# Delta rule's block inverse: products over 64 changed columns, whole array at every level, sixteens stored in both orientations

## The chip, the cores and the metric

The kernel runs on one core of a Trainium2 chip. The metric is device microseconds of one execution, the median of several runs. The engines are named as in the profile: PE is TensorE's matmul stream, PEld its weight loads, DVE is VectorE, ACT is ScalarE, POOL is GpSimd, SP is the engine that issues most DMAs. ACT issues the others.

## What is computed

A two-layer encoder over 512 tokens of width 2048. Layer 0 projects the tokens to six heads of neighbourhood attention, six heads of a bidirectional gated delta rule and four heads that attend to 256 memory tokens; it gates, concatenates and projects back. Layer 1 does the same with differential attention. The change touches only the delta rule, and in it only the solve with a triangular matrix:

```python
def gated_delta_rule_chunked(q, k, v, g, beta):      # chunks of 64 tokens
    ...
    a_mat = jnp.where(lower_strict, jnp.einsum('bhnid,bhnjd->bhnij', kb, k) * decay, 0.0)
    rhs = jnp.concatenate([v * beta[..., None], kb * jnp.exp(G)[..., None]], axis=-1)
    sol = lax.linalg.triangular_solve(a_mat + jnp.eye(C, dtype=f32), rhs, left_side=True, lower=True)
    ...
    def step(S, xs):
        v_new = u_c - jnp.einsum('bhcd,bhde->bhce', w_c, S)
        o = jnp.einsum('bhcd,bhde->bhce', qd_c, S) + jnp.einsum('bhij,bhje->bhie', qk_c, v_new)
        S = S * ge[..., None, None] + jnp.einsum('bhcd,bhce->bhde', kd_c, v_new)
```

The backward direction is the same on the flipped sequence. The kernel takes chunks of 128 tokens in place of 64 (four of them, TT = 4) and builds the inverse of I + A for each.

## The kernel before

The projections are the bulk: weights come in as float32, are split by ACT and DVE into a high and a low part (tiles wh and wl), and every projection is three matmuls. Everything else is "side work": generators that wait in five lanes. After each slot of a projection, `Lanes.step` lets the front entries of each lane emit one step, if by the planner's own count of engine time (class `Clock`) their operands are due:

```python
for e in list(q[0]):
    if e[1] + LAG > c.t["pe"]:
        continue
    c.due = 0.0
    if next(e[0], None) is None:
```

PE executes strictly in the order in which the program emits its matmuls and transposes (`MANUAL` names PE alone); the other engines' order is set by the framework's scheduler. So a side product whose operand is late holds up the projections behind it on PE.

For each delta head h, `dn_prep` (lane 2) makes A for both directions, writes it to DRAM (tile a_d), reads the 16 by 16 diagonal blocks back with one block on each partition, inverts them row by row on DVE, writes the inverses to DRAM (x_d), and reads them back as block-diagonal 128 by 128 matrices, one 128x512 tile for each direction. Then `dn_levels` (lane 4, both directions in turn) doubles the inverted blocks from 16 to 32 to 64 to 128: with N the inverse so far and Mm its transpose, N is replaced by N - Mm' (A' N masked to the new blocks). Each level needs the transpose of N (`tr4`, four PE transposes into a PSUM tile, and a copy by ACT), two sets of four products, a DVE multiply by the level's mask (tile lv, two masks for each direction) and a DVE subtraction. `mm4` does the four products at full size, 128 columns each; the last level uses 64 by 64 operands on a quarter of the array. Which of N and Mm comes from DRAM and which by transposition differs by direction, so each direction starts with a `tr4` of the tile that was loaded. `dn_rec` (lane 0) then runs the recurrence over the four chunks.

All matmuls of the block inverse are in plain float32, while the projections use fp32r. A float32 matmul stands in the trace as two MATMUL records and two LDWEIGHTS records; a transpose, or an fp32r matmul, stands as one. In a name like `pa<-w,w` the moving operand comes first, the stationary one second; the form gives the stationary size, then the output.

`zero_scratch` clears x_d once, with DMAs from SP behind which the loads of weights queue; `make_eye` fills a constant.

Of the kernel before, what the change touches and what calls it, by code (L numbers as in the profile page):

```python
# [14 lines left out]
P = 128  # L15
# [71 lines left out]
class WStream:  # L87
    """The weights in the order of their use, each unit loaded and split ahead of it."""

# [71 lines left out]
class Clock:  # L161
    """A rough count of each engine's time and of when each tile is written, so that side work is emitted
    when its operands are due."""

# [45 lines left out]
class Lanes:  # L210
    """Side work, advanced step by step between the slots of the projections."""

# [37 lines left out]
def tile_hybrid(ctx: ExitStack, tc: tile.TileContext, xT, memT, we, wo, wek, wok, weo, woo, vecs, rows, rpb,  # L250
# [63 lines left out]
    act(early, mhalf[:, 0:1], AF.Copy)  # L314
    # the array's clock rises with activity: keep it busy while the first operands come in
    warm = w2()
# [73 lines left out]

# [1 line left out]
    def run(gen):  # L392
        """Emit a projection with a step of side work behind each of its slots."""
        while True:
            try:
                next(gen)
            except StopIteration as e:
                clock.due = 0.0
                return e.value
            lanes.step()  # L400

    def chunk(hi, lo, nt, hook=None):
        """Tokens on the partitions, the weights' columns on the free axis."""
        n = W.width()
        per = 2 if n <= 256 else 1
        full = [pb() for _ in range(nt // per)]
        banks = [full[t // per][:, (t % per) * n:(t % per + 1) * n] for t in range(nt)]
        done = 0
        for k, wh, wl in W.ks():
            if hook is not None and k + 2 < KT:  # L410
                hook(k + 2)
            for t in range(nt):
                xh, xl = hi(k, t), lo(k, t)
                mm(banks[t], xh, wh, start=(k == 0 and t % per == 0), stop=False)
                mm(banks[t], xh, wl, start=False, stop=False)
                mm(banks[t], xl, wh, start=False, stop=(k == KT - 1 and t % per == per - 1))
                done += n
                if done >= SLOT and (k < KT - 1 or t < nt - 1):
                    done = 0
                    yield  # L420
        return banks

    def group(hi, lo, order=range(KT), hook=None):
        """The weights' columns on the partitions, tokens on the free axis."""
        ps = pb()
        for i, wh, wl in W.ks():
            k = order[i]
            if hook is not None:
                hook(i)
            mm(ps, wh, hi[k], start=(i == 0), stop=False)  # L430
            mm(ps, wh, lo[k], start=False, stop=False)
            mm(ps, wl, hi[k], start=False, stop=(i == KT - 1))
            if i % GS == GS - 1 and i < KT - 1:
                yield
        return ps
# [40 lines left out]

# [1 line left out]
    xh, xl = [], []  # L478
# [8 lines left out]

    # the squares follow behind the operands that the first products wait for
    late = []
# [113 lines left out]
    def mem_attention(xh, xl, rs, gq, kv, keep, hook=None):  # L603
        """rs() gives the tokens' rstd, kv() the keys and values, once the chunk has been emitted."""
        banks = run(chunk(lambda k, t: xh[k][:, t * P:(t + 1) * P], lambda k, t: xl[k][:, t * P:(t + 1) * P], 4, hook))
# [89 lines left out]

# [1 line left out]
    mix = [None] * KT  # L697
# [4 lines left out]
    def keep(i, f):  # L702
        """An output of layer 0 waits in DRAM for its gate, unless that is near."""
        if i in (5, 10, 11):
            mix[i] = f
        else:
            nc.sync.dma_start(mix_d[:, i, :], f)
            parked[i] = mix_d[:, i, :]
# [33 lines left out]
    def na_task(h, raws, vh, vl, xb):  # L742
# [7 lines left out]
        kh, kl = transposed([raws[t][:, P:2 * P] for t in range(TT)], V("na_k"))  # L750
        # relative position bias, over the scale
        tb = xb
# [6 lines left out]
        for i in range(3):  # L759
            qs = slice(64 + 128 * i, 192 + 128 * i)  # L760
            ks = slice(128 * i, 128 * i + 256)
            blocks.append((i // 2, slice((i % 2) * M, (i % 2 + 1) * M), P, qs, ks, slice(0, 256)))
        # the last eight columns of the grid, then the first eight
        for j in range(2):
# [48 lines left out]

# [1 line left out]
    NH = 12  # L815
# [14 lines left out]
    def delta_gates():  # L830
        load_ba()
        yield 1
        def t24(name):
# [5 lines left out]
                          op=ALU.add)  # L839
        # log1p(exp(-|y|)), with the rounding of 1 + e put back  # L840
        vec.scalar_tensor_tensor(ab, yb, -1.0, yb, op0=ALU.mult, op1=ALU.max)
# [41 lines left out]

    # conv weights over two (the silu takes x/2)
    cw = const.tile([P, 90], F32, name="cw")
# [48 lines left out]

    # The diagonal blocks of 16 of I + A, each on a partition: forward substitution, row by row.
    # The scratch rows of a chunk are 129 * 128 apart, so that every block is 16 * 129 after the one before.
    CS = 129 * P
    a_d = [dram.tile([2 * TT * CS], F32, name=f"a_d{i}") for i in range(2)]
    x_d = [dram.tile([2 * TT * CS], F32, name=f"x_d{i}") for i in range(2)]

# [6 lines left out]
    def zero_scratch():  # L947
        z = w2()
        nc.gpsimd.memset(z, 0.0)
        for x in x_d:  # L950
            for d in range(2):
                nc.sync.dma_start(rows_ap(x, d), v3(z, 4))

    eye16 = const.tile([64, 256], F32, name="eye16")

    def make_eye():
        nc.gpsimd.memset(eye16, 0.0)
        nc.gpsimd.memset(eye16[:, 0:256:17], 1.0)

    def dn_head(h):  # L960
# [10 lines left out]
    def dn_prep(b):  # L971
# [83 lines left out]
        for i in range(1, 16):  # L1055
            tmp = w2()[0:64, 0:i * i].rearrange("p (c j) -> p c j", c=i)
            row = g[:, 16 * i:16 * i + i].unsqueeze(1).to_broadcast([64, i, i])
            vec.tensor_tensor(tmp, row, x3[:, 0:i, 0:i], op=ALU.mult)
            vec.tensor_reduce(x[:, 16 * i:16 * i + i], tmp, AX.X, ALU.add, negate=True)
        yield 1  # L1060
        dma(blocks_ap(xd), x.rearrange("p (i j) -> p i j", i=16))
        yield 1
        inv = []
        for d in range(2):
            r = w2()
            dma(v3(r, 4), rows_ap(xd, d))
            inv.append(r)
        yield 1
        b.inv = inv

    def dn_levels(b, d):
        while b.inv is None:
            yield 1
        A = b.a[d]
        # backward, the blocks come transposed
        ips = tr4(b.inv[d])
        other = w2()
        copy(other, ips)
        N, Mm = (other, b.inv[0]) if d == 0 else (b.inv[1], other)
        for li in range(2):  # L1080
            yield 1
            if li > 0:
                mps = tr4(N)
                Mm = w2()
                copy(Mm, mps)
            pps = mm4(A, N)
            Pm = w2()
            vec.tensor_tensor(v3(Pm, 4), v3(pps, 4), cm(lv[:, d, li, :]), op=ALU.mult)
            yield 1
            nps = mm4(Mm, Pm)  # L1090
            vec.tensor_tensor(N, N, nps, op=ALU.subtract)
        yield 1
        # last level: the block between the two halves
        lo_, hi_ = slice(0, 64), slice(64, 128)
        a, c_ = (lo_, hi_) if d == 0 else (hi_, lo_)
        mps = tr4(N)
        Mm = w2()
        copy(Mm, mps)
        pps = pb()
        A4, N4, M4, p4 = v3(A, 4), v3(N, 4), v3(Mm, 4), v3(pps, 4)  # L1100
        for t in range(TT):
            mm(p4[a, t, c_], A4[c_, t, a], N4[c_, t, c_], start=True, stop=True)
        Pm = w2()
        P4 = v3(Pm, 4)
        copy(P4[a, :, c_], p4[a, :, c_])
        yield 1
        nps = pb()
        n4 = v3(nps, 4)
        for t in range(TT):
            mm(n4[a, t, c_], M4[a, t, a], P4[a, t, c_], start=True, stop=True)  # L1110
        vec.tensor_tensor(N4[a, :, c_], N4[a, :, c_], n4[a, :, c_], op=ALU.subtract)
        yield 1
# [97 lines left out]
    make_eye()  # L1210
    # masks of the doubling levels
    lv = const.tile([P, 2, 2, P], mybir.dt.bfloat16, tag="lv", name="lv")
# [12 lines left out]

    # lambda
    lp = small(2)
# [11 lines left out]

    # rotary tables times the gains: [c1 | c2] and [-s2 | s1]  # L1240
    tabs = []
# [14 lines left out]

    # out projection, residual, and the operands of layer 1
    x1_d = dram.tile([P, KT, T], F32, name="x1_d")
# [16 lines left out]

# [1 line left out]
    mix1 = [None] * KT  # L1277
# [155 lines left out]
def _layout(inputs):  # L1433
# [47 lines left out]
    def bias(first, rows_, cols):  # L1481
        """Partition (a, r), free (b, rk): the table at row difference rk - r, column difference from first + b - a."""
        a_, b_ = np.arange(rows_)[:, None, None, None], np.arange(cols)[None, None, :, None]
# [69 lines left out]
```

## Time and profile before

| | |
|---|---|
| runs | 2022.9, 2024.73, 2024.98 us; median 2024.73 |
| span of the profiled execution, first to last instruction | 2021.8 us |
| median less that span | 2.9 us |
| instructions | 27331 |

The profiled execution shows its span; what lies around the instructions is the difference to the runs, about 1 to 3 us. In the rows below, L263 is the line of every `mm`, L333 of every transpose, L205 of every DVE, ACT or POOL operation, and L340 of every DMA that ACT issues for the side work; groups are therefore told apart by tile and form.

### The profile page before, as it was taken

Reading aid. Unit: us, or ns where it says so; the run is one execution under the profiler, and the core shown is the slowest. Engines: PE = TensorE matmul, PEld = TensorE weight load, DVE = VectorE, ACT = ScalarE, POOL = GpSimd, SP = SyncE. Lnnn points to the kernel's source line nnn. Section 1 sums busy time; section 2 is a strip of 40 time slices with the busy share of each in tenths; the row PEclk is TensorE's granted clock in tenths of the full one; section 3 lists DMA queues with packets and bytes.
Section 4 is the critical chain, followed back from the end, with each engine's and each line's share of the span. In section 5 each row is a group of like instructions: output and inputs, shape, how many; then the busy total and the mean of one; then the engine's idle time right before and its main releaser. Section 6 shows DMA issues by size and latency. Waiting matters only on the chain.

```text
span 2021.8 us, 27331 instructions
## 1 busy us (share of the span) xinstructions
PE 2002.1 (99%) x10843; PEld 1741.7 (86%) x10843; DVE 1155.9 (57%) x2147; ACT 759.7 (38%) x1334; POOL 129.8 (6%) x124
## 2 busy tenths in 40 slices
PE   9999999999999999999999999999999999999999
PEld 7988899998988888888888889889899898888887
DVE  6676676767585766445334456566465656345222
ACT  5555344433343343324223343433434334223211
POOL 0100020201020202000000000100001000000000
PEclk9999999999999999999999999999999999999999
DMA  6454432222322233233444322122221222223332
GB/s 214 155 166 171 133 99 89 89 91 89 97 85 91 90 100 112 85 106 126 146 141 140 129 75 77 60 93 75 74 84 64 83 84 73 94 94 130 141 141 89
DMA packets 97503, 216.09 MB, mean 107 GB/s; under 512 B 21808, under 2 KB 36448, under 8 KB 97376
## 3 DMA queue, kind: packets, MB, share of 16 engines
q1 hardware_dynamic: 67776, 201.16, 29.1%
q10 hardware_dynamic: 29600, 13.19, 2.5%
q8 instruction: 85, 1.39, 0.3%
q14 instruction: 42, 0.34, 0.1%
HBM read 196.81 MB, written 17.51 MB: 106 GB/s over the span
## 4 chain that ended last, share of the span: by engine, by line
PE 96%; DVE 2%; DMA 1%; issue 1%; POOL 0%; ACT 0%; ACTq 0%; SPq 0%; DVEq 0%; POOLq 0%
PE pa L263 92%; PE pa L333 4%; DVE w L205 1%; DMA w<-in_xT_dram 0%; DMA w<-in_lvl_dram 0%; DVE s L205 0%; DMA w<-x_d 0%; POOL w L205 0%; DVE wl L205 0%; DVE vn L205 0%; POOL s L205 0%; DVE vb L205 0%; DVE S L205 0%; ACT wh L205 0%; ACT vd L205 0%
## 5 line engine op out<-in xcount | busy, mean ns | idle before, releaser
L205 ACT ACTIVATE wh<-wr 128x1024 fp32r<-128x1024 f32 (+3 forms) x333 | 341.7, 1027 | 720.5 <-PE pa L263 529.2
L205 DVE TENSOR_TENSOR wl<-wr,wh 128x1024 fp32r<-128x1024 f32 (+3 forms) x333 | 397.4, 1194 | 311.5 <-ACT wh L205 310.7
L263 PE MATMUL pa<-hi,wh 128*128 128x512 f32 x1312 | 518.1, 395 | 0.0
L263 PE MATMUL pa<-hi,wl 128*128 128x512 f32 x1312 | 511.6, 390 | 0.0
L263 PE MATMUL pa<-lo,wh 128*128 128x512 f32 x1312 | 511.3, 390 | 0.0
L263 PE MATMUL pa<-wh,hi 128*128 128x512 f32 (+3 forms) x1280 | 450.0, 352 | 2.4 <-ACT wh L205 2.4
L263 PE MATMUL pa<-wl,hi 128*128 128x512 f32 (+3 forms) x1280 | 439.5, 343 | 0.1
L263 PE MATMUL pa<-wh,lo 128*128 128x512 f32 (+3 forms) x1280 | 439.1, 343 | 0.0
L263 PEld LDWEIGHTS pa<-hi,wl 128*128 128x128 f32 x1312 | 246.4, 188 | 51.6
L263 PEld LDWEIGHTS pa<-hi,wh 128*128 128x128 f32 x1312 | 246.6, 188 | 49.1 <-DVE vb L205 0.5
L263 PEld LDWEIGHTS pa<-lo,wh 128*128 128x128 f32 x1312 | 246.7, 188 | 48.3
L263 PEld LDWEIGHTS pa<-wh,hi 128*128 128x128 f32 x1280 | 243.2, 190 | 23.2 <-ACT wh L205 3.2
L263 PEld LDWEIGHTS pa<-wh,lo 128*128 128x128 f32 x1280 | 242.8, 190 | 20.5
L263 PEld LDWEIGHTS pa<-wl,hi 128*128 128x128 f32 x1280 | 243.3, 190 | 19.2 <-DVE wl L205 0.6
L263 PE MATMUL pa<-w,w 128*128 128x256 f32 (+5 forms) x1416 | 191.9, 283 | 2.5 <-DVE w L205 1.6
L205 ACT ACTIVATE w<-pa 128x512 f32<-128x512 f32 (+4 forms) x234 | 123.2, 549 | 188.4 <-PE pa L333 134.6
L263 PEld LDWEIGHTS pa<-w,w 128*128 128x128 f32 (+2 forms) x1416 | 172.7, 181 | 17.1 <-issue 3.6
L205 DVE TENSOR_TENSOR w<-pa,w 128x512 fp32r<-128x512 f32 (+2 forms) x108 | 71.3, 679 | 147.9 <-PE pa L263 108.2
L205 POOL TENSOR_TENSOR s<-s,mhalf 128x1 f32<-128x1 f32 (+3 forms) x58 | 68.6, 1182 | 1190.8 <-DVE s L205 1187.8
L205 ACT ACTIVATE w<-w 128x512 f32<-128x512 f32 (+3 forms) x207 | 112.5, 578 | 55.1 <-DVE w L205 45.2
L205 ACT ACTIVATE w<-pa,s 128x256 f32<-128x256 f32 (+1 forms) x104 | 58.7, 570 | 128.8 <-DVE s L205 112.7
L333 PE MATMUL pa<-ct,w 128*128 128x128 f32 x712 | 100.4, 273 | 3.1 <-DMA w<-x_d 2.5
(148 smaller groups left out, 1461.0 us busy)
## 6 DMA issues: line engine op xcount, KB each, us to landing
wr<-in_wo_dram SPq DMA_DIRECT2D x112, 512.0 KB, 3.2
wr<-in_we_dram SPq DMA_DIRECT2D x75, 512.0 KB, 3.3
wr<-in_weo_dram SPq DMA_DIRECT2D x32, 512.0 KB, 3.2
wr<-in_woo_dram SPq DMA_DIRECT2D x32, 512.0 KB, 3.2
wr<-in_we_dram SPq DMA_DIRECT2D x40, 384.0 KB, 3.0
w<-in_xT_dram SPq DMA_DIRECT2D x32, 256.0 KB, 4.5
wr<-in_wek_dram SPq DMA_DIRECT2D x16, 512.0 KB, 4.1
wr<-in_wok_dram SPq DMA_DIRECT2D x16, 512.0 KB, 3.4
```

Of the source, the lines that this page charges most:

```text
L205: return f(*a, **k)
L263: nc.tensor.matmul(o, lhsT, rhs, start=start, stop=stop)
L333: nc.tensor.transpose(o, i, ident if idn is None else idn)
```

## The change

The inverse blocks of 16 are written to DRAM twice, as they are and transposed (x_d becomes two pairs of arrays; ACT makes the transposed copy xt), and each direction loads both N and Mm. The first `tr4` and its copy go. At every level only the 64 columns that change are multiplied: the half of N's column blocks that takes part, gathered by the access pattern `half`. The last level uses the whole 128 by 128 stationary operand like the others, and its mask is a scale of 0 or 1 for each partition (tile halves) in ACT's copy. The scratch to be cleared doubles, from four DMAs to eight. The diff also drops comments; without those:

```diff
-    x_d = [dram.tile([2 * TT * CS], F32, name=f"x_d{i}") for i in range(2)]
+    x_d = [[dram.tile([2 * TT * CS], F32, name=f"x_d{i}{j}") for j in range(2)] for i in range(2)]
...
-        for x in x_d:
+        for x in x_d[0] + x_d[1]:
             for d in range(2):
                 nc.sync.dma_start(rows_ap(x, d), v3(z, 4))
...
+    halves = const.tile([P, 2], F32, name="halves")
...
+        nc.gpsimd.memset(halves, 0.0)
+        nc.gpsimd.memset(halves[0:64, 0:1], 1.0)
+        nc.gpsimd.memset(halves[64:128, 1:2], 1.0)
...
-        yield 1
-        dma(blocks_ap(xd), x.rearrange("p (i j) -> p i j", i=16))
+        xt = w2()[0:64, 0:256]
+        copy(xt.rearrange("p (j i) -> p i j", i=16), x.rearrange("p (i j) -> p i j", i=16))
+        yield 1
+        for src, x_ in ((x, xd[0]), (xt, xd[1])):
+            dma(blocks_ap(x_), src.rearrange("p (i j) -> p i j", i=16))
         yield 1
         inv = []
         for d in range(2):
-            r = w2()
-            dma(v3(r, 4), rows_ap(xd, d))
-            inv.append(r)
+            pair = []
+            for x_ in (xd[1 - d], xd[d]):
+                r = w2()
+                dma(v3(r, 4), rows_ap(x_, d))
+                pair.append(r)
+            inv.append(pair)
...
-        ips = tr4(b.inv[d])
-        other = w2()
-        copy(other, ips)
-        N, Mm = (other, b.inv[0]) if d == 0 else (b.inv[1], other)
-        for li in range(2):
+        N, Mm = b.inv[d]
+        for li, s in enumerate((16, 32, 64)):
             yield 1
             if li > 0:
                 mps = tr4(N)
                 Mm = w2()
                 copy(Mm, mps)
-            pps = mm4(A, N)
+            def half(a, t=None):
+                a = a if t is None else a[:, t * P:(t + 1) * P]
+                return a.rearrange("p (k two s) -> p k two s", two=2, s=s)[:, :, 1 - d, :]
+            def split_cols(ap, n):
+                return ap.rearrange("p (k s) -> p k s", k=n)
+            pps = pb()
+            for t in range(TT):
+                mm(split_cols(pps[:, t * 64:(t + 1) * 64], 64 // s), A[:, t * P:(t + 1) * P], half(N, t),
+                   start=True, stop=True)
             Pm = w2()
-            vec.tensor_tensor(v3(Pm, 4), v3(pps, 4), cm(lv[:, d, li, :]), op=ALU.mult)
-            yield 1
-            nps = mm4(Mm, Pm)
-            vec.tensor_tensor(N, N, nps, op=ALU.subtract)
-        yield 1
-        lo_, hi_ = slice(0, 64), slice(64, 128)
-        a, c_ = (lo_, hi_) if d == 0 else (hi_, lo_)
-        mps = tr4(N)
-        Mm = w2()
-        copy(Mm, mps)
...
-            mm(p4[a, t, c_], A4[c_, t, a], N4[c_, t, c_], start=True, stop=True)
...
-            mm(n4[a, t, c_], M4[a, t, a], P4[a, t, c_], start=True, stop=True)
-        vec.tensor_tensor(N4[a, :, c_], N4[a, :, c_], n4[a, :, c_], op=ALU.subtract)
+            if li < 2:
+                m = half(lv[:, d, li, :]).unsqueeze(1).to_broadcast([P, TT, 64 // s, s])
+                vec.tensor_tensor(Pm[:, 0:256].rearrange("p (t k s) -> p t k s", t=TT, s=s),
+                                  pps[:, 0:256].rearrange("p (t k s) -> p t k s", t=TT, s=s), m, op=ALU.mult)
+            else:
+                copy(Pm[:, 0:256], pps[:, 0:256], halves[:, d:d + 1])
+            yield 1
+            nps = pb()
+            for t in range(TT):
+                c = slice(t * 64, (t + 1) * 64)
+                mm(nps[:, c], Mm[:, t * P:(t + 1) * P], Pm[:, c], start=True, stop=True)
+            vec.tensor_tensor(half(N), half(N), split_cols(nps[:, 0:256], 256 // s), op=ALU.subtract)
```

## Rows read from the trace of the kernel before

**Rows 1.** The page's head: span, and busy time of PE.

```profile
span 2021.8 us, 27331 instructions
...
PE 2002.1 (99%) x10843; PEld 1741.7 (86%) x10843; DVE 1155.9 (57%) x2147; ACT 759.7 (38%) x1334; POOL 129.8 (6%) x124
```

**Rows 2.** The chain that ended last, shares of the span by engine.

```profile
PE 96%; DVE 2%; DMA 1%; issue 1%; POOL 0%; ACT 0%; ACTq 0%; SPq 0%; DVEq 0%; POOLq 0%
```

**Rows 3.** Busy time by stretch: the six delta heads, 210 to 900 us.

```profile
210.00:900.00 690.00, 680.67 (x4036) 607.77 (x4035) 460.41 (x973) 262.83 (x506) 82.56 (x70) 1.00 0.30 94
```

**Rows 4.** PE groups by shape: busy us, mean ns of one record, idle before.

```profile
L263 PE MATMUL pa<-w,w 128*128 128x128 f32 x438 | 55.6, 275 | 0.0
...
L263 PE MATMUL pa<-w,w 64*64 64x64 f32 x192 | 16.2, 225 | 0.0
...
L263 PE MATMUL pa<-ct,w 128*128 128x1 f32 x48 | 5.8, 242 | 0.0
```

**Rows 5.** Timeline of weight loads: start, length of the run, count.

```profile
255.22 0.97 PEld L263 LDWEIGHTS pa<-ct,w 128*128 128x128 f32 x8
...
325.09 0.97 PEld L263 LDWEIGHTS pa<-w,w 128*128 128x128 f32 x8
...
329.46 0.54 PEld L263 LDWEIGHTS pa<-w,w 64*64 64x64 f32 x8 [0.17 <-issue]
```

**Rows 6.** The chain in order of time, 540 to 680 us: start, length, what.

```profile
627.52 0.44 PE pa L333 x4
627.96 0.89 PE pa L263 x8
```

**Rows 7.** PE's timeline around one set of last-level products, head 0.

```profile
331.54 0.34 PE L263 MATMUL pa<-wl,hi 128*128 128x384 f32 x1
331.72 0.34 PE L263 MATMUL pa<-wh,lo 128*128 128x384 f32 x1
331.99 0.68 PE L263 MATMUL pa<-w,w 64*64 64x64 f32 x8
...
332.87 0.34 PE L263 MATMUL pa<-wl,hi 128*128 128x384 f32 x1
```

**Rows 8.** Waits of PE, 210 to 900 us: total us, times, longest.

```profile
PE pa L333 <- DMA w<-x_d: 2.5, 2, 2.3
PE pa L263 <- DVE s L205: 2.4, 2, 1.2
PE pa L263 <- DVE vn L205: 2.4, 2, 1.6
```

**Rows 9.** DVE and ACT groups by shape, columns as in rows 4.

```profile
L205 ACT ACTIVATE w<-pa 128x512 f32<-128x512 f32 x110 | 64.4, 596 | 119.4 <-PE pa L333 82.3 <-PE pa L263 36.9
...
L205 DVE TENSOR_TENSOR w<-pa,lv 128x512 f32<-128x512 f32 x24 | 16.4, 689 | 23.8 <-PE pa L263 23.8
...
L205 DVE TENSOR_TENSOR w<-w,pa 64x256 f32<-64x256 f32 x12 | 5.0, 419 | 18.2 <-PE pa L263 18.2
```

**Rows 10.** DMA issues: queue, count, KB each, median us to landing.

```profile
w<-x_d ACTq DMA_DIRECT2D x12, 256.0 KB, 4.2
...
x_d<-w ACTq DMA_DIRECT2D x6, 64.0 KB, 2.5
```

**Rows 11.** PE's timeline where head 3's loaded inverses are first used.

```profile
619.43 0.63 PE L333 MATMUL pa<-ct,w 128*128 128x128 f32 x4 [2.25 <-DMA w<-x_d]
620.26 0.63 PE L333 MATMUL pa<-ct,w 128*128 128x128 f32 x4 [0.20 <-DMA w<-x_d]
```

**Rows 12.** SP's timeline where the scratch is cleared.

```profile
201.46 0.42 SPq L1214 DMA_DIRECT2D w<-in_lvl_dram  x1
201.97 4.38 SPq L952 DMA_DIRECT2D x_d<-w  x4
206.46 8.11 SPq L116 DMA_DIRECT2D wr<-in_we_dram  x2
```

**Rows 13.** ACT's timeline, use of the weights issued at 206.46.

```profile
224.60 1.06 ACT L205 ACTIVATE wh<-wr 128x1024 fp32r<-128x1024 f32 x1 [0.35 <-PE pa L263]
```

More of the change, by code (lines that the diff above doesn't have):

```diff
@@ L1085, in dn_levels @@
                 copy(Mm, mps)
-            pps = mm4(A, N)
-            Pm = w2()
-            vec.tensor_tensor(v3(Pm, 4), v3(pps, 4), cm(lv[:, d, li, :]), op=ALU.mult)
-            yield 1
-            nps = mm4(Mm, Pm)
-            vec.tensor_tensor(N, N, nps, op=ALU.subtract)
-        yield 1
-        lo_, hi_ = slice(0, 64), slice(64, 128)
-        a, c_ = (lo_, hi_) if d == 0 else (hi_, lo_)
-        mps = tr4(N)
-        Mm = w2()
-        copy(Mm, mps)
-        pps = pb()
-        A4, N4, M4, p4 = v3(A, 4), v3(N, 4), v3(Mm, 4), v3(pps, 4)
-        for t in range(TT):
-            mm(p4[a, t, c_], A4[c_, t, a], N4[c_, t, c_], start=True, stop=True)
-        Pm = w2()
-        P4 = v3(Pm, 4)
-        copy(P4[a, :, c_], p4[a, :, c_])
-        yield 1
-        nps = pb()
-        n4 = v3(nps, 4)
-        for t in range(TT):
-            mm(n4[a, t, c_], M4[a, t, a], P4[a, t, c_], start=True, stop=True)
-        vec.tensor_tensor(N4[a, :, c_], N4[a, :, c_], n4[a, :, c_], op=ALU.subtract)
+            def half(a, t=None):
[7 more added lines that the diff above has]
+                   start=True, stop=True)
+            Pm = w2()
+            if li < 2:
[4 more added lines that the diff above has]
+                copy(Pm[:, 0:256], pps[:, 0:256], halves[:, d:d + 1])
+            yield 1
+            nps = pb()
[3 more added lines that the diff above has]
+            vec.tensor_tensor(half(N), half(N), split_cols(nps[:, 0:256], 256 // s), op=ALU.subtract)
         yield 1
```

## The prediction

> **What bounds the kernel now.** I read the page's head first: PE is busy for 2002.1 of the span's 2021.8 us [rows 1]. A busy PE may still be a slow one, so the chain that ended last comes next: 96% of it is PE, and DVE and DMA hold 2% and 1% [rows 2]. In the stretch of the six delta heads PE is idle for 9.3 us of 690, at a granted clock of 1.00, while DVE is busy for 460 and ACT for 263 [rows 3]. So what the change gives or takes is counted in PE time first; DVE and ACT work counts only where a PE product waits in its fixed order for it. Those waits are few: the three largest kinds are 2.5 us for the loaded inverses and 2.4 us each for DVE in the recurrence [rows 8].
>
> What sets the price of one small product is therefore the main question, and the reader should compare runs of eight records. Eight float32 products against a 128 by 128 stationary operand with a single moving column take 0.97 us of weight loads; eight with 128 moving columns take the same 0.97 [rows 5]; the shapes of both stand in [rows 4]. On the chain eight records with 128 columns advance PE by 0.89, or 0.111 each [rows 6]. Columns between 1 and 128 are free: the load of the stationary operand sets the pace. With a 64 by 64 stationary operand eight loads take 0.54 [rows 5].
>
> **The change, part by part.** There are six heads and two directions, so twelve block inverses, and every float32 product is two records.
>
> *The first transposition goes.* Four PE transposes advance the chain by 0.44 [rows 6]; twelve of them are 5.3 us. They stand on PE itself, so all of it counts: -5.3. Their ACT copy, 0.596 each [rows 9], is not on PE's path.
>
> *Products over 64 columns at the first two levels.* Two levels, two sets of eight records, twelve inverses: 384 records with 64 columns in place of 128. The price lies between that of 1 column and that of 128, and these agree [rows 5]: 0 us. The columns are gathered in runs of 16, 32 or 64 elements, which no row shows; if the read went at half speed, 64 columns would cost as much as 128 in one piece, still under the load. I take 0, for which the cover is the weight load.
>
> *The whole array at the last level.* Now a set of eight 64 by 64 records stands between projection products thus: from 331.54 to 332.87, 1.33 us, pass three projection products of 0.18 (331.54 to 331.72) and the set, so the set costs 0.79 [rows 7]. That is more than eight loads at their own pace, because PE is idle for 0.17 at the change of shape [rows 5]. After the change the set is eight records at 0.111, or 0.89 [rows 6]. Twenty-four sets lose 0.1 each: +2.4. The lower bound is that 64 columns go at the price of the smaller operand, rival C. The Trainium skill (TensorEngine Tiling (Array Packing), Key Properties) says that a change of tiling mode drains the array; by that rule alone, with the record's price kept, the last level would gain the idle time back, and by the row the dearer load takes more than that.
>
> *DVE and ACT.* Of DVE, 48 operations shrink from about 0.69 to about 0.42 [rows 9], 13 us in all; ACT loses twelve copies of 0.596 and gains six copies of a quarter tile, below 0.596 each. Both stand beside PE, with a third and more of the stretch idle [rows 3]: 0 on the path. The cover is the projections between two steps. Where it is gone, it is a gain at most as large as the recurrence's waits, rival B. The chain inside a level gets shorter, so the recurrence starts some slots earlier.
>
> *DMA.* ACT issues one more write and two more loads for each head. The loads land about 4.2 us after issue, the write 2.5 [rows 10]. Head 3 shows what comes of lateness: PE waits 2.25 us for the first direction's inverse and, 0.83 after it, 0.20 for the second's [rows 11]. After the change the second direction's first product needs the third load of four, so about 0.83 later, and the second write adds between nothing and its whole 2.5, if it runs wholly behind the first. Against that, the first use moves one slot of the projections later, since the loop yields before its product: four products of 0.18 [rows 7], about 0.7. The sum is between -0.7 and +2.6 for a head that waits, and nothing for one with slack; one head of six waits today, and two writes issued together should run together: I take +0.5 us over all heads. Behind a waiting load on ACT's queue stand its splits of weights, which are issued well ahead (below).
>
> *Clearing the scratch.* SP issues four DMAs in 4.38 us, then the weights at 206.46 [rows 12]; eight take about 8.8, so these weights are issued 4.4 later. ACT uses them at 224.60 [rows 13], 18 us after issue, of which 13.7 would be left; 256 KB land in 4.2 [rows 10], so 512 KB in some 8.4. The cover holds: 0. If it were gone, PE would lose the 4.4. The three small fills on POOL lie beside it.
>
> *Sum.* -5.3 + 0 + 2.4 + 0.5 = -2.4 us on the profiled execution's span of 2021.8 [rows 1], or 2019.4. The median of the runs, 2024.73, is 2.9 above that span; the change does nothing outside it. Forecast: 2022.3 us. About 0.2%, here 4.05 us, is what a measurement of this kernel can tell from no change, so this counts as the same.
>
> **The rivals.**
>
> *B: the shorter level chain removes waits, and it is faster.* The recurrence's products stand in PE's order behind results of DVE, which at that time makes the next head's decay matrices; those waits and the loads' are the 7.3 us of [rows 8]. If recurrences start earlier and meet less of that work, up to the whole 7.3 goes beside the -2.9 of the products: 2014.5 at the end, about 2017 when most of it does. For it: 13 us less on DVE. Against it: the relief falls in the levels, and the waits stand later, in another head's preparation.
>
> *C: halved columns halve the products.* Then eight records go in the 0.54 of the smaller operand [rows 5] instead of 0.89 [rows 6]: 48 sets at the first levels give -16.8, and the last level falls from 24 sets of 0.79 to 24 of 0.54, -6: with -5.3 about 1997. Against it stand the two runs of 0.97 [rows 5], one with a single column. The Trainium skill (TensorE: Matmul & The Clock Gate, Back-to-back issue gap) gives a product of 64 columns about half the cycles of one of 128, which is this rival; by its own section on LDWEIGHTS the columns of the stationary operand set the load.
>
> *D: the masks' load falls behind the clearing, and it is slower.* Today SP issues the load of the level masks at 201.46, ahead of the clearing [rows 12], though the program has it behind. DVE waits for it and PE for DVE. If the order follows the program, it is issued 8.8 us later, and DVE with its splits of weights stands still for that long: up to +9, about 2031. It decides when it costs more than 6.5 us. For it: nothing but the order in the program. Against it: the first clearing DMA waits for POOL's fill now as after.
>
> *E: the shift makes more meetings, and it is slower.* The same mechanism as B turned round: a step shifted onto the next head's decay matrices waits up to 1.6 us [rows 8]. From four of the longest beyond today's (6.5 / 1.6) it decides; five give 2022.3 + 8, about 2030.
>
> **How the numbers follow.** The likeliest case is A, the sum with waits changed by at most a few us, 0.50: 2022.3, with a range of its own of 2018.5 to 2026.5; 0.04 of it lies below the bound for faster. B has 0.29, C 0.03, D 0.06, E 0.12. Faster is B, C and that part of A, 0.36; slower is D and E less 0.01 that stops short of the bound, 0.17; the same is the rest, 0.47. The range leaves out C, the last tenth of B's reach and the far part of D and E, under 0.2: 2013.5 to 2030.5.
>
> **What would show it.** In the trace after: 0.111 from record to record where 64 columns move (at about 0.07 the second step and the forecast are wrong, and C holds); 48 fewer transposes; a last-level set at 0.89 without the 0.17 of idle time; DVE's level operations near 0.42; the masks' load ahead of the eight clearing DMAs (if behind, D); PE's waits for the loaded inverses near 3 us; and its waits in the recurrence near today's (much less is B, much more is E).

## The result and the profile after

| | before | after |
|---|---|---|
| median of runs | 2024.55 us (4 runs) | 2035.12 us (4 runs, 2031.32 to 2038.15) |
| span of the profiled execution | 2021.8 us | 2032.3 us |
| ratio of medians, 95% interval | | 1.0053 [1.004, 1.0065] |

The changed kernel is slower by 0.5%. The forecast of 2022.3 us was wrong, and the result lies above its range. The page's head and the shares of the chain answer to [rows 1, 2]:

```profile
span 2032.3 us, 27280 instructions
...
PE 2004.4 (99%) x10795; PEld 1746.7 (86%) x10795; DVE 1145.1 (56%) x2147; ACT 757.2 (37%) x1328; POOL 132.5 (7%) x127
...
PE 92%; DVE 4%; issue 1%; ACT 1%; DMA 1%; POOL 0%; ACTq 0%; SPq 0%; DVEq 0%; POOLq 0%
```

PE has 48 records fewer, the twelve transposes of four. What is new is in the chain: PE falls from 96% to 92%, and DVE rises from 2% to 4%. The chain now leaves PE more often, so PE waits more.

**Where the 10 us are.** Set the same projection product of both traces side by side: at 308 us the kernel after is 0.03 us behind, at the end of the delta heads (917 us of before) 10.35, at the end of the program 10.54. So the whole loss lies in the six heads. In the windows view (stretch, its length, then busy time of PE, PEld, DVE, ACT and POOL, granted clock, and the DMA columns) PE is idle for 9.3 us of 720 before and for 17.8 after; first line before, second after:

```profile
210.00:930.00 720.00, 710.67 (x4168) 632.64 (x4167) 472.09 (x986) 271.15 (x516) 82.56 (x70) 1.00 0.30 95
210.00:930.00 720.00, 702.19 (x4075) 630.12 (x4074) 457.88 (x982) 265.44 (x506) 85.06 (x70) 1.00 0.32 99
```

Between the products at 308 and at 917 us I gave every PE record the time from its own start to the start of the next. The sums, before and after: transposes 35.4 and 29.7 us; the levels' products 60.3 and 66.1; the recurrence's products 48.6 and 53.8; the projections 442.9 and 446.4; all else 21.8 and 23.4. The projections hold about 2.2 us less, since 24 changes of array shape are gone (0.27 in place of 0.18 from the last projection record to the set, [rows 7]). So the work of the change is -5.7 + 5.8 - 2.2 = -2.1 us (the 5.8 still holds one wait of 0.8 for the loads), and what is left, about +12.5, is waits and what comes with them. PE's idle time grew by 8.5 of it. Another 1.7, an estimate from half of 3.4, is the clock: behind the second of the two long waits below, the granted clock is 0.50, that is 1.2 GHz in place of 2.4, for 3.4 us, in which a projection product follows the one before it after 0.32 us in place of 0.175:

```profile
656.00:659.40 3.40, 3.40 (x13) 3.40 (x12) 0.00 (x0) 0.00 (x0) 0.00 (x0) 0.50 0.00 0
```

The remaining 2 us or so I did not split. The clock by itself is not the cause of the loss: the four runs of the kernel after had mean granted clocks of 0.996 to 0.999, and against the mean of the runs of before at the same value (58 runs, beside the experiments below) they are slower by 8.6 to 9.8 us.

The view of PE's waits, 210 to 920 us, columns as in [rows 8]:

```profile
PE pa L263 <- DVE w L205: 6.9, 2, 3.5
PE pa L263 <- DVE vn L205: 3.4, 7, 1.0
PE pa L263 <- DVE vb L205: 1.6, 3, 1.1
PE pa L333 <- DVE vb L205: 1.5, 2, 0.8
PE pa L263 <- DMA w<-x_d: 0.8, 1, 0.8
```

Before, the largest three were 2.5, 2.4 and 2.4 [rows 8]. The loads' wait fell from 2.5 to 0.8. Two waits of 3.5 us for a DVE tile `w` are new, and the many small ones for `vn` and `vb`, which belong to the recurrence.

**The two long waits.** The chain in order of time around the first of them (start, length, what):

```profile
444.70 0.45 PE pa L333 x4
...
445.17 0.60 ACT w L205
...
445.80 0.70 DVE s L205
...
446.77 1.68 POOL s L205
...
448.48 0.70 DVE w L205
...
449.32 4.51 PE pa L263 x28
```

Four transposes (the next head's keys), ACT's square of them, DVE's sum, POOL's inverse root, DVE's scaling, and then PE goes on. This is `dn_prep` of the next head. But PE's timeline shows what it goes on with:

```profile
445.50 0.38 PE L263 MATMUL pa<-vb,w 128*128 128x128 f32 x2
449.32 0.68 PE L263 MATMUL pa<-S,w 128*128 128x128 f32 x4 [3.44 <-DVE w L205]
```

That is a product of the recurrence with the state `S`, and no operand of it is made by that scaling. ACT had last written `S` at 443.54. What they share is the place: in the built program the product's output tile lies in the PSUM bank that holds the transposed keys, and their last reader is the scaling, in DVE's timeline:

```profile
448.48 0.69 DVE L205 TENSOR_TENSOR w<-pa,s 128x512 f32<-128x512 f32 x1 [0.90 <-POOL s L205]
```

So PE stood for 3.6 us, counted from the end of two records of 0.111, because it had nowhere to write; run 3 tests this. The same happens at 654.83 with another bank.

**What went as forecast.** A set of eight records with 64 columns, and the load that sets its pace, in PE's and PEld's timelines:

```profile
325.11 1.00 PE L263 MATMUL pa<-w,w 128*128 128x64 f32 x8
325.95 0.60 PE L333 MATMUL pa<-ct,w 128*128 128x128 f32 x4
```

```profile
325.00 0.97 PEld L263 LDWEIGHTS pa<-w,w 128*128 128x128 f32 x8
```

The run of eight loads takes the 0.97 of [rows 5], whether 128 columns, one, or 64 move. A last-level set after:

```profile
336.06 0.33 PE L263 MATMUL pa<-wh,lo 128*128 128x384 f32 x1
336.23 1.00 PE L263 MATMUL pa<-w,w 128*128 128x64 f32 x8
337.04 0.42 PE L263 MATMUL pa<-wh,hi 128*128 128x384 f32 x1
337.30 0.33 PE L263 MATMUL pa<-wl,hi 128*128 128x384 f32 x1
```

From 336.06 to 337.30, 1.24 us, pass two projection products of 0.175 and the set: 0.89, against 0.79 in [rows 7]. DVE's level operations shrank as well, from the 689 ns of [rows 9] to 423 (the groups by shape):

```profile
L205 DVE TENSOR_TENSOR w<-pa,lv 128x256 f32<-128x256 f32 x24 | 10.1, 423 | 20.7 <-PE pa L263 20.7
```

In SP's timeline the masks' load is still ahead of the eight clearing DMAs, so rival D did not occur:

```profile
201.27 0.42 SPq L1221 DMA_DIRECT2D w<-in_lvl_dram  x1
201.79 7.94 SPq L952 DMA_DIRECT2D x_d<-w  x8
209.83 10.60 SPq L116 DMA_DIRECT2D wr<-in_we_dram  x3
```

### The profile page after: what moved, and what is told of

Read it like the earlier page. It is cut to its first block, busy times and chain, and to the rows that moved or that the text cites. A ratio compares the mean times of both kernels' runs of the same rounds, so it can differ in the third digit from the quotient of the medians.

```text
span 2032.3 us, 27280 instructions
## 1 busy us (share of the span) xinstructions
PE 2004.4 (99%) x10795; PEld 1746.7 (86%) x10795; DVE 1145.1 (56%) x2147; ACT 757.2 (37%) x1328; POOL 132.5 (7%) x127
## 3 DMA queue, kind: packets, MB, share of 16 engines
q1 hardware_dynamic: 69888, 202.21, 29.7%
## 4 chain that ended last, share of the span: by engine, by line
PE 92%; DVE 4%; issue 1%; ACT 1%; DMA 1%; POOL 0%; ACTq 0%; SPq 0%; DVEq 0%; POOLq 0%
PE pa L263 89%; PE pa L333 3%; DVE w L205 2%; DVE wl L205 1%; ACT wh L205 1%; POOL s L205 0%; DMA w<-x_d 0%; ACT w L205 0%; DMA w<-in_lvl_dram 0%; DMA w<-in_xT_dram 0%; DVE lo L205 0%; DVE s L205 0%; DVE vn L205 0%; DVE acc L205 0%; DVE vb L205 0%
## 5 line engine op out<-in xcount | busy, mean ns | idle before, releaser
L263 PEld LDWEIGHTS pa<-lo,wh 128*128 128x128 f32 x1312 | 246.6, 188 | 48.6
L263 PE MATMUL pa<-w,w 128*128 128x256 f32 (+5 forms) x1416 | 199.9, 288 | 4.5 <-ACT w L205 1.8
L263 PEld LDWEIGHTS pa<-w,w 128*128 128x128 f32 (+1 forms) x1416 | 184.8, 190 | 14.9 <-ACT w L205 2.9
L205 ACT ACTIVATE w<-pa 128x512 f32<-128x512 f32 (+3 forms) x210 | 112.3, 557 | 170.4 <-PE pa L333 110.4
L333 PE MATMUL pa<-ct,w 128*128 128x128 f32 (+1 forms) x664 | 93.9, 273 | 3.2 <-DVE vb L205 1.5
```

The costliest lines, as they stand in the source:

```text
L205: return f(*a, **k)
L263: nc.tensor.matmul(o, lhsT, rhs, start=start, stop=stop)
L333: nc.tensor.transpose(o, i, ident if idn is None else idn)
```

## The theory and the experiments

**The theory.** The change moves the order of PE's instructions, and the new order meets more waits than its work saves. The order comes from the planner's charge for a product (n columns):

```python
clock.on("pe", max(n / 2.4, 106.0) if rhs.dtype == F32R else max(4 * n / 2.4, 100.0), [o], [lhsT, rhs])
```

A float32 product of 128 columns is charged 213 ns, one of 64 columns 107. The chip takes two records of 0.111, 222 ns, for either. Since the change the planner believes the levels cheaper than they are, and it no longer charges the first `tr4`; so it emits side steps at other slots. It counts operands only, not PSUM banks. **Rivals:** the work itself costs more than was summed (gathered columns, whole array), or the loads and the doubled scratch do.

**1. The change's work in the order of before.** Each new instruction is charged as the one that it replaces, and the missing `tr4` too, on names behind which nothing is emitted; PE's order is then that of before, less the transposes (in the two traces PE's records follow in the same order, but for the 48 transposes).

```diff
+        ips, other = pb_name(d), (N, Mm)[d]
+        for _ in range(TT):
+            clock.on("pe", 109.0, [ips], [(Mm, N)[d]])
+        clock.on("act", 180.0 + 0.83 * 512, [other], [ips])
...
-                   start=True, stop=True)
+                   start=True, stop=True, ns=4 * (P if li < 2 else 64) / 2.4)
...
+            clock.on("vec", 75.0 + 1.05 * (512 if li < 2 else 256), [N], [N, nps])
```

> All of the change's work, but the planner is charged for each step of the levels as before, so PE gets its products in the old order (less the first transpositions). Theory order (the planner's cheaper steps move side work to slots where PE's products wait for a PSUM bank or for DVE; the work by itself is 2.5 us less on PE): about 2022 us, no waits of 3.6 us on PE. Rival loads (four loads and two writes for each head come late): about 2035, with PE waiting for the loaded inverses. Rival products (the whole-array products cost PE more than counted): about 2035, with PE's waits as few as before.

Measured: 2024.53 us against 2024.88 for before, ratio 0.9994 [0.9984, 1.0005]. The order alone is worth 10.6 us, and both rivals fall as its cause: work, loads and scratch are all in this run. But the gain of the work is not kept either. PE's timeline at head 3, and below it the lines of the windows view for the 10.2 us that follow, of this run and of before:

```profile
619.51 1.07 PE L265 MATMUL pa<-w,w 128*128 128x64 f32 x8 [1.37 <-DMA w<-x_d]
621.93 1.94 PE L265 MATMUL pa<-w,w 128*128 128x64 f32 x8 [1.34 <-DMA w<-x_d]
...
622.00:632.20 10.20, 10.20 (x46) 10.10 (x47) 4.44 (x8) 1.44 (x2) 0.00 (x0) 0.50 0.01 4
...
622.00:632.20 10.20, 10.20 (x88) 10.15 (x88) 8.13 (x13) 2.78 (x5) 0.00 (x0) 1.00 0.20 67
```

Four loads are issued between 613.9 and 615.4 and land at 619.4, 621.1, 621.9 and 622.6. The first direction's first product waits for the first of them, the second direction's for the third. PE waits twice, 2.7 us, where [rows 11] had 2.25 and 0.20, and from one projection product to the same one later the stretch around head 3 lasts 4.2 us longer than before's. The waits themselves are only 0.3 us longer. The rest is the clock: from 622 to 632 us the granted clock is 0.50 (1.2 GHz), and the set of eight at 621.93 takes 1.94 us where the one at 619.51 took 1.07. Half of 10.2 us is an estimate of about 5 us lost, less 0.9 for the two groups of transposes that are gone there. In the trace before, the same place has a wait of 2.25 us too, but a clock of 1.00. The ten runs fit this: two had a mean granted clock of 1.000 and took 2019.2 and 2019.3 us, 4 us less than the two runs of before at 1.000 (2023.2 and 2023.3); the other eight, at 0.996 and 0.997, took 2023.5 to 2027.5. So by these figures the work's gain is there, and is lost again when the clock falls at the late loads. No run changes the clock alone, and why it fell here and not in the trace before is open.

**2. The work of before in the order of after.** The reverse: before's instructions, charged as after's.

```diff
-            pps = mm4(A, N)
+            pps = mm4(A, N, 4 * 64 / 2.4)
...
-            nps = mm4(Mm, Pm)
+            nps = mm4(Mm, Pm, 4 * 64 / 2.4)
...
-        copy(other, ips)
+        nc.scalar.activation(other, ips, AF.Copy, bias=0.0, scale=1.0)
+        clock.ready[other.tensor.name] = clock.ready[f"charged_load{d}"]
```

> All of the work of the kernel before, first transpositions included, but the planner is charged as in the changed kernel, so PE gets its products in the new order. Theory order: about 2037 us (the changed kernel's 2035 plus the 2.5 us of PE work that the change saves), with waits of several us on PE in the recurrence. Rivals loads and products: about 2024.5, as before, since neither loads nor products are changed.

Measured: 2039.8 against 2024.88, ratio 1.0073 [1.0057, 1.0089], 2.8 us above the expectation; PE's records follow as in the trace after, with the 48 transposes more. The new order makes the old work 14.9 us slower, with the same wait in PE's timeline:

```profile
448.00 0.38 PE L265 MATMUL pa<-vb,w 128*128 128x128 f32 x2
451.82 0.68 PE L265 MATMUL pa<-S,w 128*128 128x128 f32 x4 [3.43 <-DVE w L205]
```

Runs 1 and 2 together separate the two effects: order +10.6 to +14.9, work 0 to -5.

**3. The bank freed.** The kernel after, and ACT copies the transposed keys out of their bank; the square and the scaling read the copy. The copy isn't charged (`same` tells the planner that the copy is ready when its source is), so PE's order stays that of after.

```diff
+        kc = w2()
+        nc.scalar.activation(kc, kps, AF.Copy, bias=0.0, scale=1.0)
+        same(kc, kps)
+        kps = kc
```

> The changed kernel, except that ACT copies the transposed keys out of their PSUM bank at once (one 128x512 copy more for each head, not charged to the planner, so the order is the changed kernel's), and the norm and the scaling read the copy. Theory order in its narrow form (two waits of 3.6 us for that bank): both vanish, about 2028 us. Rival: the bank is only the last of several waits at that place and PE waits for the next one instead, about 2035. Rivals loads and products: 2035.

Measured: 2024.83 against 2024.88, ratio 0.9994 [0.9984, 1.0005], so 10.3 us less than after, and 3 us less than expected. PE's timeline at the place of the long wait:

```profile
445.60 0.38 PE L263 MATMUL pa<-vb,w 128*128 128x128 f32 x2
445.92 0.71 PE L263 MATMUL pa<-S,w 128*128 128x128 f32 x4
```

The same product follows after 0.32 us instead of 3.82, with the scaling as late as ever. So it waited for the bank and not for the scaling's result. Set side by side product by product (PE's order is the same), the trace of this run gains 3.5 us at the first place and 5.1 at the second. Of these the two waits are 7, and 1.7 is the clock, which does not fall behind the second place in this run (in the heads it falls once, at 572 us). The two profiled executions differ by 8.7 us in all; the rest of the 10.3 between the medians is not accounted for.

**4. Old order, and before's last level.** Run 1 with the 64 by 64 operands on a quarter of the array.

```diff
-        for li, s in enumerate((16, 32, 64)):
+        for li, s in enumerate((16, 32)):
...
+        for t in range(TT):
+            mm(p4[a, t, c_], A4[c_, t, a], N4[c_, t, c_], start=True, stop=True)
```

> As the run with all work in the old order, but the last level is that of the kernel before (64 by 64 operands on a quarter of the array). Theory order with the prices read from the traces: 2.4 us less than all work in the old order, about 2019.5 us. If the whole array is no dearer than the quarter: the same time as all work in the old order. Rivals loads: about 2033.

Measured: 2023.31 against 2024.88, ratio 0.9991 [0.9981, 1.0001]; 1.2 us less than run 1, where the rows of both kernels give 2.4. The expectation was missed by about 4 us, and the loads' waits are larger still, 3.8 us; here too the granted clock is 0.50 at head 3, from 621.1 to 631.3 us. The medians alone don't settle the size of the last level. The two traces do, since PE's order is the same in both: from the projection product or transpose ahead of a set to the second one behind it, each of the 24 sets is 0.08 to 0.09 us shorter on the quarter, 2.1 us in all.

**5. Both orientations loaded, and nothing else.** Before with four loads, no first `tr4`, products at full size, old order.

```diff
-        ips = tr4(b.inv[d])
-        other = w2()
-        copy(other, ips)
-        N, Mm = (other, b.inv[0]) if d == 0 else (b.inv[1], other)
+        N, Mm = b.inv[d]
```

> The kernel before with one part of the change alone: both orientations stored and loaded, the first transpositions gone, all products at their old size, the planner charged as before so that the order is the old one. What the run with all work in the old order showed (4.2 us lost where head 3 waits for its loads): 5.3 us of transpositions less, some 4 to 5 us of lateness more, about 2024, with PE waiting 4 us or more for the loaded inverses in head 3. If that lateness was chance: about 2019.5. If two more loads cost every head: over 2028.

Measured: 2022.23 against 2023.77, ratio 0.9989 [0.9981, 0.9998]. The transposes were worth 5.3 us in the sum; 1.5 are left. The loads' waits are 4.3 us in three waits, two of them, 3.6 us, in head 3 (before: 2.5 in all). So the first expectation is nearest, 1.8 us too high, and the lateness is no cost of every head. Waits longer by 1.8 us don't eat 3.8 by themselves: in head 3 the granted clock is 0.50 again, from 619.8 to 626.5 us.

**6. Old order, both mends.** Run 4, with the loads that are needed first issued first and the bank freed as in run 3.

```diff
-        for d in range(2):
-            pair = []
-            for x_ in (xd[1 - d], xd[d]):
+        inv = [[], []]
+        for k in range(2):
+            for d in range(2):
                 r = w2()
-                dma(v3(r, 4), rows_ap(x_, d))
+                dma(v3(r, 4), rows_ap(xd[1 - d if k == 0 else d], d))
+                inv[d].append(r)
```

> A candidate to beat both: both orientations loaded, old order, products of 64 columns, last level on a quarter of the array; besides, the two tiles that the first products read are loaded ahead of the two that come later, and ACT copies the transposed keys out of their bank. If head 3's lateness comes from the third load standing behind a second that is not yet needed: some 1 to 2 us less than the same without these, about 2021. If it comes from the second write and the bandwidth of four loads: about 2023.

Measured: 2015.93 against 2023.77, ratio 0.9961 [0.9948, 0.9974]. That is 5 us below the lower of the two figures expected. With the waits mended the work's gain shows: PE is idle for 6.4 us from 210 to 930, for loads 1.5. The run makes two edits at once, so their shares aren't separated. The granted clock is 0.50 from 616.8 to 626.9 us here too, behind the one wait for loads that is left; the only one of the six runs with a mean granted clock of 1.000 took 2012.2 us.

**7. Before, with the bank freed.** The copy of run 3 in the kernel before.

> The kernel before in its own order, with the one edit that freed the bank in the changed kernel. Theory order: that edit only takes back a wait that the new order made, and the old order has none there, so about 2024.5. Rival: the bank is a standing cost of either order, so 8 to 10 us less, about 2015.

Measured: 2021.65 against 2023.77, ratio 0.9988 [0.998, 0.9997]. Before's order has two bank waits of its own, the DVE `s` 2.4 us of [rows 8], and they are gone. (In the built program the product that waits lies in the bank that DVE's update of `S` still reads; with the keys copied out it lies in the bank that the keys have left.) That is 2 us, between theory and rival, not 10, and not nothing: the copy is no general gain of 10, it mends what an order meets.

**8. The planner told the price.** The kernel after, one number changed.

```diff
-        clock.on("pe", max(n / 2.4, 106.0) if rhs.dtype == F32R else max(4 * n / 2.4, 100.0), [o], [lhsT, rhs])
+        clock.on("pe", max(n / 2.4, 106.0) if rhs.dtype == F32R else max(4 * n / 2.4, 213.3), [o], [lhsT, rhs])
```

> The changed kernel, with the planner charged at least 213 ns for every float32 product, whatever its columns (the chip takes 222). Theory order says only that the order changes again; if the waits come from steps that the planner takes to be done too early, the 3.6 us waits vanish and the time is between 2022 and 2027; if the old order was merely luckier, the time is anywhere between 2022 and 2037, and the waits stand at other places.

Measured: 2016.07 against 2023.77, ratio 0.9963 [0.9949, 0.9977], and 19 us less than after, by a change that emits the same work; it is 6 us below the range expected. PE's waits, 210 to 920 us:

```profile
PE pa L263 <- DVE vn L205: 3.5, 4, 1.6
PE pa L263 <- DMA w<-x_d: 1.0, 1, 1.0
PE pa L263 <- ACT w L205: 0.7, 1, 0.7
```

No bank wait of 3.5 us is left.

**9. Price, bank and loads together.** Runs 8, 3 and the loads' order of 6.

> The changed kernel with the planner's true price (order as in that run), the keys copied out of their bank, and the first needed loads issued first. If bank and loads are what is left there (about 1 us of loads, 0.4 to 1 us of single banks): 1 to 3 us less than the true price alone, about 2014. If the true price has already taken these waits away: the same 2016.

Measured: 2014.83 against 2024.57, ratio 0.9951 [0.9936, 0.9965]. PE's idle time is 4.5 us; the loads are waited for no more.

**10. The same with the last level on a quarter.** Run 9 and the edit of run 4.

> The same with the last level on a quarter of the array, as in the kernel before. By the prices in the traces (0.79 against 0.89 for a set of eight records, 24 sets) 2.4 us less than the run beside it, if the order stays alike; the planner is charged 0.85 for a set in both. If the order decides: anywhere within 8 us of it.

Measured: 2009.76 against 2024.57, ratio 0.9932 [0.9916, 0.9948]. It is the fastest of all, 14.8 us below before and 25.4 below after. It is 5.1 us below run 9, where the sets' 0.10 gives 2.4. The order does not decide it: PE's records follow as in run 9. In this order two sets stand together five times, and there the quarter gains more; PE's timelines, run 9 first:

```profile
331.82 1.89 PE L263 MATMUL pa<-w,w 128*128 128x64 f32 x16
333.52 0.42 PE L263 MATMUL pa<-wh,hi 128*128 128x384 f32 x1
...
329.37 0.96 PE L263 MATMUL pa<-w,w 64*64 64x64 f32 x16
330.27 0.44 PE L263 MATMUL pa<-wh,hi 128*128 128x384 f32 x1
```

Sixteen records go from 1.70 us to 0.90. With the projection products around it such a pair is 0.69 shorter, a single set 0.09, which makes 5 * 0.69 + 14 * 0.09 = 4.7 us. Another part is a wait at 208 us, ahead of the delta heads, which was 2.2 us in run 9's profile and 0.2 in this one; it differs from kernel to kernel without a pattern that I found (1.1 before, 1.4 after). Together they make about the 6.7 us between the two profiled executions.

**11. Before, told the price.** Is the right price a gain in itself?

> The kernel before with the same charge of at least 213 ns for each float32 product; there only the last level's products (charged 107, they take about 200 with the change of shape) and the products with one column change their charge. If a true price is good in itself: some us less than before, about 2018 to 2022. If an order is luck: on either side of 2024, up to 10 us off.

Measured: 2025.02 against 2024.57, ratio 1.0001 [0.999, 1.0012]. No: the order changes, the loads are waited for no more, and other waits take the place, in the view of PE's waits:

```profile
PE pa L263 <- DVE vn L205: 8.4, 10, 2.8
```

**12. After, everything emitted later.** `LAG`, what the planner adds before it lets a step go, from 200 to 1200 ns.

> The changed kernel, with every side step emitted 1.2 us after its operands are due by the planner, in place of 0.2. If the waits are for operands that come a little late: most of them vanish, about 2022 or less. If they are for PSUM banks, which the planner does not count: waits of a bank remain somewhere, and the time is between 2022 and 2035 with PE waiting for DVE's reads of other tiles than the operands.

Measured: 2016.22 against 2024.57, ratio 0.9961 [0.9948, 0.9975]. A blunt shift does as well as the right price. PE's idle time from 210 to 930 us is 8.4 us; the longest waits left are 2.8 and 2.2 us, and the 2.2 is again a bank: a level's product waits for the scaling of another head's keys, whose bank it takes in the built program.

## Why the prediction was wrong, point by point

- *The first transposition goes, -5.3:* right in PE's work (35.4 to 29.7 us). In run 5 1.5 of it reach the end, while the loads are late and the clock falls behind them.
- *64 columns at the first two levels, 0:* right. The load of the stationary operand sets the pace: 0.97 for eight, as for 1 and 128 columns. Rival C falls. The Trainium skill (TensorE: Matmul & The Clock Gate, Back-to-back issue gap) has a table in which an isolated product of 64 columns takes about half the cycles of one of 128; in this stream, where each record has a load of its own, that doesn't show. By the formula of the Trainium skill (TensorE: Matmul & The Clock Gate, LDWEIGHTS), which counts the columns of the stationary operand alone, 128 columns make an estimate of 107 ns; the trace has 111 to 112.
- *The whole array at the last level, +2.4:* right in size where a set stands alone, 0.89 against 0.79 (runs 1 and 4: 2.1 us for 24 sets). The 0.17 of [rows 5] that the prediction gives to PE is idle time of the weight loads, PEld; on PE the change of shape shows as about 0.09 ahead of the set [rows 7].
- *DMA, +0.5:* near for the kernel after, where the loads' wait is 0.8 in place of 2.5, but only because the new order puts the first product elsewhere. In the old order, for which I summed it, the wait grew to between 3.3 and 4.3 (runs 1, 4, 5), by 0.8 to 1.8 us: more than the 0.5, and inside my bounds of -0.7 to +2.6. The lateness hits one head twice, once for each direction. What the sum lacked is the clock: around these waits it stood at 0.50 for 6.7 to 10.2 us, by the estimate under run 1 some 3 to 5 us, more than the waits themselves grew.
- *Clearing, masks:* right; the eight clearing DMAs take 7.94 us in place of the 8.8 summed, and the masks' load stays ahead of them.
- *The failed step is the last sign of "What would show it", "its waits in the recurrence near today's", and with it case A.* PE's idle time in the heads went from 9.3 to 17.8 us, 6.9 of it in two waits for a PSUM bank. I took the waits as a property of the work and allowed for few meetings more or fewer. Runs 1, 2 and 3 show that they are a property of the order: the same work is 10.6 us faster in the old one, and the old work 14.9 slower in the new.
- *Rival E* named the right sign and the right pair, the recurrence against the next head's preparation, and its 2030 is near the 2035 (rival D's 2031 is nearer, but its cause did not occur). It had two things wrong. The wait is for a PSUM bank and not for DVE's time; and the price of a meeting was taken from the longest wait for DVE that the trace before showed, 1.6 us, where a bank held through square, sum, POOL's root and scaling costs 3.6. That row could have been bounded: the next head's keys were transposed, squared and scaled before as well, so the length of their hold on a bank stood in the trace (548.84 to 553.42, 4.6 us, from the transposes to the end of the scaling), only with no long wait behind it.
- *Rival B* could have occurred by the same mechanism. Runs 8 and 12 are about 2016 us, with the work of after unchanged: 19 us lie between orders of one work. So the sign of this change hung on an order that neither the diff nor the profile of before shows.

Open is why just this order meets the long bank waits, and whether it could be told ahead: run 11 shows that a truer price is no remedy by itself. The variation of the wait at 208 us and the falls of the clock were not tested by themselves.

## What to carry to other kernels

Where a planner sets the order, a change of what an instruction is charged is a change of the order everywhere behind it: price the change once with the old order held and once with the old work in the new order, before judging the change. When PE waits for an instruction that makes none of its operands, look at which tile shares its PSUM bank; copying a tile out that waits for a long chain is cheap (here one ACT copy for each head: -10.3 us in the order of after, -2.1 in that of before). When a wait costs more than it lasts, read the granted clock behind it. The Trainium skill (Perfetto Trace Analysis, Optimization Strategy) says that the same gap repeated on the busiest engine can mean that there is no room for the next tile; here it was the same 3.4 to 3.5 us gap at two heads.

## What was not expected of the hardware

A set of eight float32 records took 0.97 us of loads with 1, 64 or 128 moving columns, so halving the columns gave PE nothing. The smaller operand of 64 by 64 takes 0.54 for eight loads [rows 5], but a set costs 0.79 with the change of shape around it: against the whole array's 0.89 it gains 0.1, not 0.4. Two such sets together take 0.90 for sixteen records, against 1.70 on the whole array (runs 9 and 10). Behind two waits of 1.4 and 1.3 us PE's clock stood at half, 1.2 GHz, for 10.2 us (run 1), which cost more than the two waits; a wait of 2.25 us in the trace before and one of 3.44 us in the trace after (449 us) were not followed by a fall. Four loads of 256 KB issued together by one engine landed 0.7 to 1.7 us apart (619.4, 621.1, 621.9, 622.6 in run 1), so the order in which they are issued can itself be worth a wait.
